# The MLP's second product by Strassen's seven products, over all features, in rings of buffers

## The chip, the cores and the metric

The kernel runs on 1 core of one Trainium2 chip. The metric is the device time of one execution in microseconds (us). A difference of about 0.3% is what a measurement of this kernel can tell from none.

## The reference

Two layers act on 1024 tokens of width 1024, all in float32. Each layer is a token mixer, a cross-attention into 256 memory tokens and a squared-ReLU MLP, each followed by a layer norm of a scaled residual. The change is in the MLP:

```python
def squared_relu_mlp(x, w1, w2):
    h = jnp.square(jax.nn.relu(jnp.einsum('bsd,df->bsf', x, w1)))
    return jnp.einsum('bsf,fd->bsd', h, w2)

for l in range(DEPTH):      # DEPTH = 2
    ...
    ff = squared_relu_mlp(x, w_ff1[l], w_ff2[l])
    x = layer_norm(ALPHA * x + ff, ln3_g[l], ln3_b[l])
```

Here `x` is 1024 x 1024, `w1` is 1024 x 4096 and `w2` is 4096 x 1024.

## The kernel before

Every float32 factor is split into two fp32r parts, a high and a low one: ScalarE copies the high part, and VectorE or GpSimd subtracts it to get the low part (`split`, L648 on the line of the subtraction). `mm3` (L333 to L335) then adds three TensorE products into one PSUM bank: high by high, high by low, low by high. A bank is 128 x 512; there are eight. SBUF is handed out by an allocator of the kernel's own (`Arena`), and all loads and stores are issued by SyncE's one queue.

The stages of a layer that matter here, in order:

- `out_proj(..., "values", ...)` is the output product of the cross-attention, token tile by token tile (8 tiles of 128 tokens). It ends each tile with a layer norm (`layer_norm`, L620 and L623 on VectorE).
- `x_combos` takes each normed tile, stores it to DRAM (`x2`), transposes it on TensorE (L1522) and makes the token-side operands of the first product: B11 and B21 from tiles 0 to 3 alone, and B22, T1, T2, T3, T4 from tile t and tile t - 4 together (L1540 to L1550 on VectorE, the splits of T1 to T3 on GpSimd).
- `up` is the first product, h = relu(w1 x) squared, already by Strassen's algorithm with Winograd's sums: 16 chunks of 256 features, seven products of 12 matmuls each (`PRODUCTS`). Products 1 and 2 need B11 and B21 only. The order is: 1 and 2 of the first four chunks (`UP_FIRST`), then 6, 5, 7, 3, 4 of these, then the other chunks whole. The weights are loaded by chunk and summed (S1 to S4, L1581); VectorE adds the products (L1672), ScalarE squares, and four 128 x 512 tiles per chunk are stored to `h` in DRAM.
- `mlp` then makes the second product plainly. For each of 8 groups of 512 features, `fetch` loads four 128 x 1024 rows of h and splits them (L1694 ScalarE, L1695 VectorE), the weights of w2 come through a small prefetcher (L283 to L285), and `down(g, t, d)` makes 12 matmuls into one bank and adds them to the residual tile (L1737 in group 0, L1741 after). In the last group it goes tile by tile, so that the layer norms of one tile run beside the products of the next.

What is written is not what runs in order: a scheduler places each engine's instructions by priorities, so that the program's order of one engine is a result of it. The orders below are those of the built programs.

## Time and profile before

| | |
|---|---|
| median of 3 runs | 3144.88 us (3141.48 to 3149.49) |
| profiled execution | 3145.91 us |
| its span | 3144.1 us |
| TensorE busy | 2979.4 us, 95% of the span, 14824 matmuls |
| VectorE busy | 1913.4 us, 61% |
| ScalarE, GpSimd busy | 1410.7 us (45%), 1367.0 us (43%) |
| mean granted TensorE clock | 0.973 of full |

In the profile PE is TensorE's matmuls, PEld its weight loads, DVE VectorE, ACT ScalarE, POOL GpSimd and SP SyncE. Matmuls are pipelined: one of 128 x 512 shows about 390 ns, but the next one starts 0.23 us after it, so the pace is read from counts over a stretch, not from mean durations. The profiled execution took 3145.91 us, 1.8 us more than its span.

### The profile page before, as it was taken

To read this page: it belongs to the slowest core of one execution; us is meant where nothing else is said; L and a number is where in the kernel's file an instruction comes from. 1 tells how busy PE (TensorE), PEld (TensorE's weight loads), DVE (VectorE), ACT (ScalarE), POOL (GpSimd) and SP (SyncE) were. 2 spreads that over 40 slices of the span, in tenths; PEclk is the share of its full clock that TensorE was granted. 3 is DMA by queue.
4 is the path that set the end of the run, shared out by engine and by line. 5 is a ranking of instruction groups with operands and counts; after the bars stand their busy time and mean duration, and the time that the engine had idled before them with its cause. 6 is when DMAs were issued, how large, how long until landed. Compare 5 with 4: busy or idle time off the path is not lost. (4 is left out here: it accounts for less than half of the span.)

```text
span 3144.1 us, 42269 instructions
## 1 busy us (share of the span) xinstructions
PE 2979.4 (95%) x14824; PEld 2521.0 (80%) x14824; DVE 1913.4 (61%) x3983; ACT 1410.7 (45%) x2794; POOL 1367.0 (43%) x1292
## 2 busy tenths in 40 slices
...
DVE  5899888662675344333658998875526754443446
...
PEclk9998899999989999999999988999999899999999
...
GB/s 122 54 42 58 54 113 96 131 94 60 115 81 111 111 111 207 98 103 95 88 50 69 28 59 61 125 93 124 84 92 90 74 110 112 108 209 85 114 91 64
DMA packets 201398, 297.49 MB, mean 95 GB/s; under 512 B 16865, under 2 KB 123361, under 8 KB 201185
## 3 DMA queue, kind: packets, MB, share of 16 engines
...
## 5 line engine op out<-in xcount | busy, mean ns | idle before, releaser
L333 PE MATMUL banks<-sb,sb 128*128 128x512 f32 (+3 forms) x3904 | 1470.7, 379 | 25.6 <-DVE sb L648 11.7
L334 PE MATMUL banks<-sb,sb 128*128 128x512 f32 (+3 forms) x3904 | 1468.3, 377 | 4.6 <-POOL sb L285 4.6
L335 PE MATMUL banks<-sb,sb 128*128 128x512 f32 (+3 forms) x3904 | 1464.9, 377 | 0.5 <-POOL sb L648 0.5
L285 POOL TENSOR_TENSOR sb<-sb,sb 128x512 fp32r<-128x512 f32 (+2 forms) x416 | 572.8, 1392 | 963.0 <-ACT sb L284 674.8
L333 PEld LDWEIGHTS banks<-sb,sb 128*128 128x128 f32 x3904 | 740.3, 190 | 161.6 <-DVE sb L648 13.5
L334 PEld LDWEIGHTS banks<-sb,sb 128*128 128x128 f32 x3904 | 740.2, 190 | 133.0 <-POOL sb L285 6.4
L335 PEld LDWEIGHTS banks<-sb,sb 128*128 128x128 f32 x3904 | 739.0, 189 | 130.1 <-POOL sb L648 1.2
L648 POOL TENSOR_TENSOR sb<-sb,sb 128x512 fp32r<-128x512 f32 (+1 forms) x316 | 399.0, 1281 | 516.1 <-ACT sb L647 453.1
L284 ACT CAST sb<-sb 128x512 fp32r<-128x512 f32 (+2 forms) x320 | 190.3, 608 | 454.4 <-PE banks L335 283.1
L1741 DVE TENSOR_TENSOR sb<-banks,sb 128x512 f32<-128x512 f32 x224 | 153.4, 689 | 312.9 <-PE banks L335 311.8
L647 ACT CAST sb<-sb 128x512 fp32r<-128x512 f32 (+1 forms) x340 | 191.4, 588 | 287.9 <-PE banks L334 115.4
L1672 DVE TENSOR_TENSOR sb<-banks,sb 128x512 f32<-128x512 f32 x224 | 151.2, 688 | 230.4 <-PE banks L335 218.4
L647 ACT CAST sb<-banks 128x384 fp32r<-128x384 f32 (+2 forms) x324 | 160.6, 516 | 168.9 <-PE banks L1522 81.9
L648 DVE TENSOR_TENSOR sb<-banks,sb 128x384 fp32r<-128x384 f32 (+2 forms) x324 | 187.3, 594 | 69.3 <-ACT sb L647 65.1
L796 DVE TENSOR_SCALAR_CACHE_REDUCE sb<-sb,sb 128x768 bf16<-128x768 f32 (+3 forms) x256 | 207.4, 810 | 3.2 <-POOL sb L752 0.3
L997 POOL TENSOR_SCALAR sb<-sb,sb 128x128 f32<-128x128 f32 (+7 forms) x192 | 146.5, 778 | 75.5 <-DVE sb L995 70.4
L986 ACT ACTIVATE sb<-sb,sb 128x128 f32<-128x128 f32 (+7 forms) x192 | 141.8, 739 | 80.5 <-DVE sb L980 74.2
L792 ACT ACTIVATE sb<-sb,sb 128x1024 bf16<-128x1024 f32 (+1 forms) x128 | 140.4, 1097 | 47.0 <-DVE sb L815 45.6
L1694 ACT CAST sb<-sb 128x1024 fp32r<-128x1024 f32 x64 | 67.3, 1051 | 162.6 <-DMA sb<-h 84.3
L1057 PE MATMUL banks<-sb,sb 128*128 128x320 f32 (+4 forms) x288 | 83.1, 389 | 53.4 <-DVE sb L980 40.7
L1695 DVE TENSOR_TENSOR sb<-sb,sb 128x1024 fp32r<-128x1024 f32 x64 | 93.0, 1457 | 63.6 <-ACT sb L1694 62.6
L1634 ACT ACTIVATE sb<-sb 128x512 f32<-128x512 f32 x128 | 80.8, 631 | 111.7 <-DVE sb L1672 111.5
...
## 6 DMA issues: line engine op xcount, KB each, us to landing
sb<-w_ff_dram SPq DMA_DIRECT2D x128, 256.0 KB, 3.0
sb<-w_ff_dram SPq DMA_DIRECT2D x64, 512.0 KB, 3.8
h<-sb SPq DMA_DIRECT2D x128, 256.0 KB, 2.0
sb<-h SPq DMA_DIRECT2D x64, 512.0 KB, 4.1
sb<-w_in_dram SPq DMA_DIRECT2D x64, 256.0 KB, 2.9
sb<-w_mkv_dram SPq DMA_DIRECT2D x64, 256.0 KB, 2.7
xs<-sb SPq DMA_DIRECT2D x24, 512.0 KB, 2.6
sb<-xs SPq DMA_DIRECT2D x24, 512.0 KB, 3.9
```

What stands on the lines that cost most here:

```text
L284: (k.nc.vector.tensor_copy if self.late else k.nc.scalar.copy)(hi, st)
L285: k.nc.gpsimd.tensor_tensor(lo, st, hi.bitcast(F32), op=ALU.subtract)
L333: mm(out, lh, rh, start=start, stop=False)
L334: mm(out, lh, rl, start=False, stop=False)
L335: mm(out, ll, rh, start=False, stop=stop)
L647: nc.scalar.copy(hi, src)
L648: eng.tensor_tensor(lo, src, hi.bitcast(F32), op=ALU.subtract)
L796: nc.vector.tensor_scalar(junkb[:, :w], x, c, None, op0=ALU.is_ge, op1=ALU.add, accum_out=n)
L986: nc.scalar.activation(pt.ap, pt.ap, AF.Exp, bias=mn, scale=-1.0, accum_out=sm)
L997: nc.gpsimd.tensor_scalar(pt.ap, pt.ap, rc[:, i : i + 1], 0.0, op0=ALU.mult, op1=ALU.add)
L1672: nc.vector.tensor_tensor(r.ap, ps.ap, part[c, x].ap, op=ALU.add)
L1741: nc.vector.tensor_tensor(x, ps.ap, x, op=ALU.add)
```

## The change

The second product is made by Strassen's seven products too. It is cut in halves three ways: tokens (tiles 0 to 3 and 4 to 7), features (rows 256c to 256c + 127 and the 128 after them, for each chunk c), and output columns (512 and 512). `up` now stores, in place of the four quarters of h, the seven combinations that are the left factors of the seven products (`LEFT`): two quarters themselves and five sums or differences, made on VectorE (L1685) and stored as 128 x 512 tiles. `mlp` then goes product by product (5, 7, 3, 1, 4, 6, 2), each over all 16 chunks into four banks. Step n of 112 loads one tile of h and one of w2, adds or subtracts another quarter of w2 where the product asks for it (L1790), splits both factors (L645, which is `split`'s subtraction, L648 before) and makes 4 x 3 = 12 matmuls (four token tiles, three products each). All buffers come from rings: tiles as loaded (`raws`, 8 of 512 columns, so four steps), split pairs (`pairs`, `DOWN_AHEAD` = 7 steps) and quarters of w2 that a later product needs again (`slots`). At the end of a product its four banks are added to one or two residual tiles each (`ADDS`, L1845 and L1847). Token tiles 0 to 3 are final after product 4 and normed under product 6; the last eight steps of product 2 go tile by tile.

`UP_FIRST` is 6 instead of 4, so products 1 and 2 of six chunks come first, with small loads of their own for A11 and A12 (L1607). `out_proj` hands back the last four tiles, and their transposes and sums are called for between the first products of `up`.

```diff
-UP_FIRST = 4
+UP_FIRST = 6
+DOWN_AHEAD = 7
...
+        if hold:
+            return pend
...
+            left[c] = {"A22", "S1", "S2", "S3", "S4"}
+            if c >= UP_FIRST:
+                left[c] |= {"A11", "A12"}
...
+            early = c < UP_FIRST and n in ("A11", "A12")
+            if early:
+                b = sb.alloc(512)
+                src = b.ap.rearrange("p (k f) -> p k f", k=4)
+                i = 4 * (int(n[2]) - 1)
+                nc.sync.dma_start(src, v[:, i : i + 4, 256 * c : 256 * c + P])
...
+    LEFT = {
+        1: ("11", "+", "22"), 2: ("21", "+", "22"), 3: ("11",), 4: ("22",),
+        5: ("11", "+", "12"), 6: ("21", "-", "11"), 7: ("12", "-", "22"),
+    }
+    ADDS = {
+        1: ((0, 0, 1), (1, 1, 1)), 2: ((1, 0, 1), (1, 1, -1)), 3: ((0, 1, 1), (1, 1, 1)),
+        4: ((0, 0, 1), (1, 0, 1)), 5: ((0, 0, -1), (0, 1, 1)), 6: ((1, 1, 1),),
+        7: ((0, 0, 1),),
+    }
+
+    def h_rows(self, p, c):
+        r = ((p - 1) * (DFF // 256) + c) * P
+        return self.h[r : r + P, :]
...
-            r = 256 * c + P * f
-            nc.sync.dma_start(self.h[r : r + P, half * 512 : half * 512 + 512], b.ap)
...
+            if c < UP_FIRST and n == "11":
+
+                nc.sync.dma_start(self.h_rows(3, c), b.ap)
+                sb.free(b)
+                return
+            if c < UP_FIRST and n == "22":
+                first = quads[c, "11"] = sb.alloc(512)
+                nc.sync.dma_start(first.ap, self.h_rows(3, c))
+            quads[c, n] = b
+            have = {x for c_, x in quads if c_ == c}
+            for p, spec in self.LEFT.items():
+                names = spec[::2]
+                if (n in names or (n == "22" and c < UP_FIRST and "11" in names)) and have >= set(names):
+                    if len(names) == 1:
+                        if names[0] == n:
+                            nc.sync.dma_start(self.h_rows(p, c), b.ap)
+                        continue
+                    x, y = (quads[c, m].ap for m in names)
+                    z = sb.alloc(512)
+                    nc.vector.tensor_tensor(
+                        z.ap, x, y, op=ALU.add if spec[1] == "+" else ALU.subtract
+                    )
+                    nc.sync.dma_start(self.h_rows(p, c), z.ap)
+                    sb.free(z)
...
+            if pend and i in (0, 1, 2, 4):
+                combos(*pend.pop(0))
...
-        def fetch(g, i):
-            f = sb.alloc(1024)
-            r = (4 * g + i) * P
-            nc.sync.dma_start(f.ap, self.h[r : r + P, :])
-            b = [sb.alloc(1024) for _ in range(2)]
-            nc.scalar.copy(b[0].r, f.ap)
-            nc.vector.tensor_tensor(b[1].r, f.ap, b[0].r.bitcast(F32), op=ALU.subtract)
-            sb.free(f)
-            hs[g, i] = b
...
+        steps = [(p, i) for p in (5, 7, 3, 1, 4, 6, 2) for i in range(nk)]
...
+        def prepare(n):
+            if n >= len(steps) or n in have:
+                return
+            p, i = steps[n]
+            x, own = take(raws, 2 * n, 512)
+            y, _ = take(raws, 2 * n + 1, 512)
+            load(x, self.h_rows(p, i))
+            add = nc.vector.tensor_tensor
+            if p == 5:
+                src = load(y, w2(1, 1, i))
+                kept[i] = slots[i] if slots else sb.alloc(512)
+                nc.scalar.copy(kept[i].ap, y.ap)
+            elif p == 2:
+                src = kept.pop(i)
+            else:
+                src = y
+                row, col, op = {
+                    7: (1, 0, ALU.add), 3: (0, 1, ALU.subtract), 1: (0, 0, ALU.add),
+                    4: (1, 0, ALU.subtract), 6: (0, 1, ALU.add),
+                }[p]
+                if p == 1:
+                    new = load(slots[(i - 2) % len(slots)], w2(0, 0, i))
+                    add(y.ap, new.ap, kept[i].ap, op=op)
+                    kept[i] = new
+                else:
+                    load(y, w2(row, col, i))
+                    add(y.ap, y.ap, kept[i].ap, op=op)
+            res = []
+            for j, (b, eng) in enumerate(
+                ((x, nc.gpsimd if i % 2 else nc.vector), (src, nc.vector))
+            ):
+                hl, _ = take(pairs if n < nlast else None, 2 * n + j, 1024)
+                self.split(hl.r[:, :512], hl.r[:, 512:], b.ap, eng=eng)
+                res.append(hl)
+            if not own:
+                sb.free(x)
+                sb.free(y)
+            if p == 2:
+                slots.remove(src)
+                sb.free(src)
+            have[n] = res
...
+        pairs += [b for n in range(first) for b in have[n]]
+        pairs += [sb.alloc(1024) for _ in range(2 * (DOWN_AHEAD - first))]
+        raws += [sb.alloc(512) for _ in range(8)]
+        slots += [kept[i] for i in range(first)]
+        slots += [sb.alloc(512) for _ in range(nk + 2 - first)]
...
-        def down(g, t, d):
-            ps = self.ps.alloc()
-            for i in range(4):
-                u = self.wi[f"f2_{g}", l][4 * d + i]
-                hi, lo = self.w.get(u)
-                h = hs[g, i]
-                self.mm3(ps.ap, h[0].r[:, s], h[1].r[:, s], hi, lo, i == 0, i == 3)
...
+        def product(n, t, ps):
+            i = steps[n][1]
+            x, y = (b.r for b in have[n])
             s = slice(t * P, (t + 1) * P)
+            self.mm3(
+                ps[t].ap, x[:, :512][:, s], x[:, 512:][:, s], y[:, :512], y[:, 512:],
+                i == 0, i == nk - 1,
+            )
...
+        def evict(p, t, ps):
+            for half, d, sign in self.ADDS[p]:
+                tt = 4 * half + t
+                x = xs[tt].ap[:, d * 512 : d * 512 + 512]
+                op = ALU.add if sign > 0 else ALU.subtract
+                if (tt, d) in begun:
+                    nc.vector.tensor_tensor(x, x, ps[t].ap, op=op)
+                else:
+                    nc.vector.scalar_tensor_tensor(
+                        x, x, ALPHA, ps[t].ap, op0=ALU.mult, op1=op
+                    )
+                    begun.add((tt, d))
...
+        for n, (p, i) in enumerate(steps[:nlast]):
+            for m in range(n, min(2 * n + 5, n + DOWN_AHEAD)):
+                prepare(m)
+            if p in (5, 7) and i in (6, 8, 10, 12):
+                t = i // 2 - 3 + (0 if p == 5 else 4)
+                nc.sync.dma_start(xs[t].ap, self.x2[t * P : (t + 1) * P, :])
+            if p == 3 and i == 0:
+                self.ln_consts("ln3_g", "ln3_b", l, gb)
+            if i == 0:
+                ps = [self.ps.alloc() for _ in range(4)]
+            for t in range(4):
+                product(n, t, ps)
+            drop(n)
+            if i == nk - 1:
+                for t in range(4):
+                    evict(p, t, ps)
+            if p == 6:
+                if i % 4 == 2:
+                    norm(i // 4, 0)
...
+        for n in range(nlast, len(steps)):
+            prepare(n)
...
+        for t in range(4):
+            for n in range(nlast, len(steps)):
+                product(n, t, ps)
+                if t == 3:
+                    drop(n)
+            evict(2, t, ps)
+            norm(4 + t, 2 if t < 1 else int(t < 3))
```

TensorE, at the start of layer 0's `up`, before. L1522 are the transposes of the last token tiles (`sb_67` is the identity), the rows around them the last matmuls of `out_proj` and the first of product 1:

```order
L333 MATMUL banks<-sb_673,sb_178 128x512
L334 MATMUL banks<-sb_673,sb_178 128x512
L335 MATMUL banks<-sb_673,sb_5643 128x512
L1522 MATMUL banks<-sb_67,sb_7490 128x128 x8
L1522 MATMUL banks<-sb_67,sb_3604 128x128 x8
L1522 MATMUL banks<-sb_67,sb_1853 128x128 x8
L333 MATMUL banks<-sb_86,sb_2723 128x512
L334 MATMUL banks<-sb_93,sb_2723 128x512
```

The same place now (L340 to L342 are `mm3`, L1521 the transposes), here the end of the first product and the second of the four tiles:

```order
L340 MATMUL banks<-sb_86,sb_1731 128x512
L341 MATMUL banks<-sb_93,sb_1731 128x512
L342 MATMUL banks<-sb_86,sb_1731 128x512
L1521 MATMUL banks<-sb_67,sb_3604 128x128 x8
L340 MATMUL banks<-sb_169,sb_310 128x512
L341 MATMUL banks<-sb_7550,sb_310 128x512
L342 MATMUL banks<-sb_169,sb_310 128x512
```

Before, tiles 4, 5 and 6 are transposed in one piece behind `out_proj`, then come 48 matmuls, then tile 7. Now tile 4 follows `out_proj`, tiles 5 and 6 come after 12 matmuls each, and tile 7 after 74 more, 98 in all.

VectorE, around the end of the layer norm of token tile 7 (L623, its last operation, and L589 and L591 before it), before. L1581 are sums of weights, L648 splits, L1672 sums of products, L1540 the first operation on the transposed tile 7:

```order
L1581 TENSOR_TENSOR sb_905<-sb_4403,sb_195 128x512
L648 TENSOR_TENSOR sb_7831<-sb_3887,sb_7830 128x4x128
L589 TENSOR_SCALAR sb_2510<-sb_2510 128x1
L648 TENSOR_TENSOR sb_7831<-sb_7871,sb_7830 128x4x128
L1672 TENSOR_TENSOR sb_2551<-banks,sb_4592 128x512
L591 TENSOR_SCALAR sb_2510<-sb_2510 128x1
L1581 TENSOR_TENSOR sb_4403<-sb_2195,sb_7490 128x512
L589 TENSOR_SCALAR sb_2510<-sb_2510 128x1
L591 TENSOR_SCALAR sb_2510<-sb_2510 128x1
L623 SCALAR_TENSOR_TENSOR sb_1937<-sb_1937,sb_2510,sb_135 128x1024
L1581 TENSOR_TENSOR sb_2551<-sb_2111,sb_905 128x512
L1540 TENSOR_TENSOR sb_2690<-banks,sb_86 128x512
```

The same place now (L620 is the norm's last operation, L645 the splits, L1582 the sums of weights, L1727 the sums of products, L1539 the first operation on tile 7):

```order
L645 TENSOR_TENSOR sb_177<-banks,sb_170 128x4x128
L586 TENSOR_SCALAR sb_2510<-sb_2510 128x1
L1549 TENSOR_TENSOR sb_842<-sb_842,sb_7550 128x512
L588 TENSOR_SCALAR sb_2510<-sb_2510 128x1
L645 TENSOR_TENSOR sb_7830<-sb_7861,sb_7829 128x4x128
L620 SCALAR_TENSOR_TENSOR sb_5765<-sb_5765,sb_2510,sb_135 128x1024
L645 TENSOR_TENSOR sb_7830<-sb_842,sb_7829 128x4x128
L1727 TENSOR_TENSOR sb_842<-banks,sb_7910 128x512
L1582 TENSOR_TENSOR sb_7963<-sb_163,sb_2111 128x512
L1539 TENSOR_TENSOR sb_901<-banks,sb_86 128x512
L1582 TENSOR_TENSOR sb_8083<-sb_7963,sb_163 128x512
L1542 TENSOR_TENSOR sb_901<-sb_901,sb_93 128x512
```

Before, three sums of weights stand between tile 7's last products and the end of its norm; now none does, and one of the three splits of T4 has moved behind the norm too.

VectorE in the second product of layer 0, before: sums into the residual (L1741) and splits of fetched rows of h (L1695):

```order
L1741 TENSOR_TENSOR sb_9930<-banks,sb_9930 128x512
L1695 TENSOR_TENSOR sb_1747<-sb_149,sb_1731 128x1024
L1741 TENSOR_TENSOR sb_9932<-banks,sb_9932 128x512
L1695 TENSOR_TENSOR sb_4838<-sb_10741,sb_3222 128x1024
L1741 TENSOR_TENSOR sb_9922<-banks,sb_9922 128x512
L1695 TENSOR_TENSOR sb_5442<-sb_1763,sb_7222 128x1024
```

The same engine now, under product 6 of layer 0: sums of w2 (L1790), splits (L645) and, between them, the norms of token tiles 0 to 3 (L604 to L617):

```order
L617 SCALAR_TENSOR_TENSOR sb_7489<-sb_7489,sb_2510,sb_10747 128x1024
L604 BN_AGGR sb_2510<-sb_2510 128x2
L1790 TENSOR_TENSOR sb_3520<-sb_3520,sb_842 128x512
L645 TENSOR_TENSOR sb_629<-sb_2551,sb_629 128x512
L604 BN_AGGR sb_2510<-sb_2510 128x2
L1790 TENSOR_TENSOR sb_10137<-sb_10137,sb_905 128x512
L579 TENSOR_SCALAR sb_2510<-sb_2510 128x1
L581 TENSOR_SCALAR sb_2510<-sb_2510 128x1
L617 SCALAR_TENSOR_TENSOR sb_5317<-sb_5317,sb_2510,sb_10747 128x1024
L645 TENSOR_TENSOR sb_729<-sb_901,sb_729 128x512
```

The operations with a PSUM operand (`banks`) have become rare there, and most of what VectorE now does has both inputs in SBUF (`sb`).

## Rows read from the trace of the kernel before

**Rows 1.** The page: busy time, then the span in 40 equal slices (tenths busy of VectorE, and the granted TensorE clock in tenths).

```profile
PE 2979.4 (95%) x14824; PEld 2521.0 (80%) x14824; DVE 1913.4 (61%) x3983; ACT 1410.7 (45%) x2794; POOL 1367.0 (43%) x1292
...
DVE  5899888662675344333658998875526754443446
...
PEclk9998899999989999999999988999999899999999
```

**Rows 2.** The view by stretches, in the MLP's two products of both layers: the stretch, its length, then busy time and count of instructions of each engine, the granted clock, the DMA share and GB/s.

```profile
950.00:1180.00 230.00, 230.00 (x1016) 190.51 (x1015) 100.72 (x140) 117.05 (x197) 112.19 (x88) 1.00 0.34 112
1260.00:1500.00 240.00, 240.00 (x1060) 198.80 (x1059) 91.50 (x110) 47.44 (x65) 69.65 (x47) 1.00 0.28 96
2510.00:2750.00 240.00, 240.00 (x1061) 198.72 (x1060) 108.72 (x148) 123.44 (x208) 121.01 (x93) 1.00 0.33 110
2810.00:3080.00 270.00, 270.00 (x1193) 223.58 (x1192) 100.91 (x123) 55.97 (x76) 76.17 (x51) 1.00 0.27 91
```

**Rows 3.** The same view around the start of `up`, in layer 0, layer 1, and two pieces of the first.

```profile
872.00:940.00 68.00, 50.42 (x219) 40.99 (x218) 54.85 (x75) 27.74 (x50) 39.61 (x26) 0.87 0.23 74
2440.00:2510.00 70.00, 50.14 (x202) 39.55 (x201) 49.14 (x67) 28.85 (x51) 38.24 (x25) 0.80 0.22 75
908.00:912.00 4.00, 0.00 (x0) 0.00 (x0) 4.00 (x8) 2.31 (x5) 0.82 (x2) 0.65 0.42 133
912.00:916.00 4.00, 0.00 (x0) 0.00 (x0) 3.49 (x7) 1.75 (x3) 2.55 (x2) 0.50 0.35 131
```

**Rows 4.** The view of waits of TensorE, from 872 to 940 us (first two) and from 2440 to 2510 us (last): who waited for whom, us in total, times, longest.

```profile
PE banks L1522 <- DVE sb L623: 10.4, 1, 10.4
PE banks L333 <- DVE sb L648: 5.7, 1, 5.7
...
PE banks L1522 <- DVE sb L623: 10.0, 1, 10.0
```

**Rows 5.** The timeline of layer 0 between `out_proj` and `up`: start, length, engine, line, and in brackets the idle time before and what ended it.

```profile
883.78 1.37 DVE L1300 SCALAR_TENSOR_TENSOR sb<-sb,banks 128x512 f32<-128x512 f32 x2 [3.55 <-PE banks L335]
884.27 2.78 PE L1522 MATMUL banks<-sb,sb 128*128 128x128 f32 x24
...
890.54 17.80 POOL L648 TENSOR_TENSOR sb<-sb,sb 128x512 fp32r<-128x512 f32 x11 [1.25 <-ACT sb L647]
...
915.56 1.28 DVE L623 SCALAR_TENSOR_TENSOR sb<-sb,sb,sb 128x1024 f32<-128x1024 f32 x1
...
916.90 1.97 PE L1522 MATMUL banks<-sb,sb 128*128 128x128 f32 x8 [10.39 <-DVE sb L623]
```

**Rows 6.** Groups of instructions by line from 890.5 to 907 us, where VectorE and GpSimd both run without a pause: count, busy time, mean ns of one.

```profile
L1549 DVE TENSOR_TENSOR sb<-sb,sb 128x512 f32<-128x512 f32 x3 | 4.1, 1362 | 0.0
...
L1545 DVE TENSOR_TENSOR sb<-banks,sb 128x512 f32<-128x512 f32 x3 | 2.0, 674 | 0.0
...
L648 POOL TENSOR_TENSOR sb<-sb,sb 128x512 fp32r<-128x512 f32 x11 | 17.8, 1653 | 1.2 <-ACT sb L647 1.2
```

**Rows 7.** Operations of one kind: the view of line L1581 over the whole span (ns, least/median/most), and groups by line from 950 to 1180 us (L1672, L1581, L648, L647) and from 1260 to 1500 us (L285).

```profile
L1581 DVE TENSOR_TENSOR sb<-sb,sb x96: 676/693/1807, 905.4 to 2748.1; 128x512 f32<-128x512 f32 x96
...
L1672 DVE TENSOR_TENSOR sb<-banks,sb 128x512 f32<-128x512 f32 x88 | 59.5, 689 | 92.8 <-PE banks L335 91.5 <-ACT sb L1635 1.2
L1581 DVE TENSOR_TENSOR sb<-sb,sb 128x512 f32<-128x512 f32 x39 | 31.6, 811 | 24.6 <-DMA h<-sb 12.8 <-ACT sb L1634 8.5 <-ACT sb L1635 2.7
...
L648 POOL TENSOR_TENSOR sb<-sb,sb 128x512 fp32r<-128x512 f32 x88 | 114.3, 1318 | 117.8 <-ACT sb L647 117.8
...
L647 ACT CAST sb<-sb 128x512 fp32r<-128x512 f32 x88 | 52.4, 621 | 61.3 <-PE banks L334 44.1 <-DVE sb L1581 14.5 <-DMA h<-sb 2.3
...
L285 POOL TENSOR_TENSOR sb<-sb,sb 128x512 fp32r<-128x512 f32 x47 | 70.8, 1531 | 169.6 <-ACT sb L284 139.4 <-issue 17.3 <-PE banks L334 12.7
```

**Rows 8.** VectorE's groups from 1530 to 1580 us, where layer 0's last norms run: the pieces of a norm, and of a transposed tile's split (L639).

```profile
L596 DVE BATCH_NORM_STATS2 sb<-sb 128x6 f32<-128x512 f32 x14 | 9.6, 688 | 0.1
...
L639 DVE TENSOR_TENSOR sb<-banks,sb 128x512 fp32r<-128x512 f32 x12 | 8.1, 683 | 0.5 <-ACT sb L638 0.5
L589 DVE TENSOR_SCALAR sb<-sb 128x1 f32<-128x1 f32 x23 | 6.1, 266 | 0.3
L591 DVE TENSOR_SCALAR sb<-sb 128x1 f32<-128x1 f32 x23 | 4.8, 208 | 0.3
...
L607 DVE BATCH_NORM_AGGREGATE sb<-sb 128x2 f32<-128x12 f32 x8 | 1.6, 203 | 0.1
```

**Rows 9.** DMA issues with KB each and median us to landing: from 1260 to 1500 us (first two), and the busiest stretch, from 1190 to 1240 us (its rate, then two issues).

```profile
sb<-w_ff_dram SPq DMA_DIRECT2D x47, 256.0 KB, 2.8
sb<-h SPq DMA_DIRECT2D x20, 512.0 KB, 3.4
...
DMA packets 5447, 15.20 MB, mean 304 GB/s; under 512 B 601, under 2 KB 601, under 8 KB 5445
...
sb<-x SPq DMA_DIRECT2D x8, 512.0 KB, 8.6
sb<-w_ff_dram SPq DMA_DIRECT2D x11, 256.0 KB, 6.0
```

**Rows 10.** The timeline at the end of the kernel: the last matmul, and VectorE's last operation on the last token tile.

```profile
3130.91 0.39 PE L335 MATMUL banks<-sb,sb 128*128 128x512 f32 x1
...
3139.22 1.28 DVE L623 SCALAR_TENSOR_TENSOR sb<-sb,sb,sb 128x1024 f32<-128x1024 f32 x1
```

177 lines of the change are left out of this document (83 added, 94 removed).

## The prediction

> **What bounds the kernel now.** I read the page first, then the view by stretches, then the waits and the timeline where that view shows a hole. The page has TensorE at 95% and VectorE at 61% [rows 1]. By stretches, TensorE is busy all the time in both products of the MLP, in both layers, at a granted clock of 1.00, and the pace is the same everywhere: 240 us / 1060 = 0.2264 us per 128 x 512 matmul, also 230 / 1016 and 270 / 1193 [rows 2]. VectorE is at 38 to 45% there. So in the MLP the end moves with the number of matmuls, as long as nothing else becomes late. There is one hole per layer, between `out_proj` and `up`: the stretches of 68 and 70 us hold 219 and 202 TensorE instructions at clocks of 0.87 and 0.80 [rows 3]. 32 of each are transposes at 2.78 / 24 = 0.116 us [rows 5]. Work there is 187 x 0.2264 + 3.7 = 46.0 us and 170 x 0.2264 + 3.7 = 42.2 us, so 22.0 and 27.8 us are lost. The waits name the cause: TensorE stands 10.4 and 10.0 us before tile 7's transposes, for the end of its layer norm on VectorE [rows 4], which runs without a pause from tile 7's products at 883.78 to that end at 916.84 [rows 5]. After eight idle microseconds the clock is at 0.50, the lower of its levels, 1.2 GHz [rows 3].
>
> **A. Fewer matmuls.** Before, 8 groups x 16 x 12 = 1536 per layer; now 7 x 16 x 12 = 1344. In two layers 384 x 0.2264 = 86.9 us go, since TensorE had no pause there [rows 2].
>
> **B. The hole.** In the new order tile 7's transposes stand behind 24 others (2.8 us) and 98 matmuls (22.2 us), so at the earliest at 884.3 + 25.0 = 909.3. On VectorE three sums of weights and one split of T4 have left the way to the norm's end; with GpSimd at work beside them they took 1.36 each, and one without it 0.69 [rows 6, 7]: 3 x 1.36 + 0.69 = 4.8 us, so the norm ends at about 912. GpSimd decides a little too. The eighth weight pair's split stands behind eight of the nine splits of T1 to T3; the last of these waits for VectorE's 27th operation, at some 907, and at 1.65 us each [rows 6] the pair is ready near 912, where TensorE wants it at 906. So TensorE stops for 5 to 6 us there instead of 10 + 6 later, and the 46 matmuls left (10.4 us) then cover tile 7's sums. With 3 to 4 us at the lower clock I take 10 us lost in layer 0 and 13 in layer 1 (its hole is a quarter deeper). Gain: 12 + 14.8 = 27 us. Bounds: 0 (the hole moves to the next wait) and 42 us (4 left in each).
>
> **C. VectorE under product 6.** This is the change's dearest new place, because the norms of tiles 0 to 3 now run among the splits. An operation on 512 columns takes 0.69 us with a PSUM input [rows 7] and as much at its median without [rows 7], but 1.36 where GpSimd runs beside it, while those with PSUM stay at 0.67 [rows 6]. A GpSimd split of 1.65 us covers 1.65 / 1.36 = 1.2 such operations, so it costs VectorE up to 1.2 x 0.67 = 0.8 us. A plain step pair in the second product is 2 sums, 3 splits and its share of 8 sums into the residual (one): 6 x 0.69 + 0.8 = 4.9 us against TensorE's 24 x 0.2264 = 5.43. So VectorE follows, and gets the full lead of six steps. From the sums after product 4 to the last split before the tile-by-tile end, the new order holds on VectorE 40 splits, 9 sums of w2 and 12 sums into the residual (61 x 0.69 = 42.1), four norms at 0.69 + 0.2 + 4 x 0.27 + 4 x 0.21 + 2 x 1.28 = 5.4 [rows 5, 8] (21.5), and in layer 0 six splits of transposed tiles at 0.68 [rows 8] (4.1): 67.7 us, with 13 GpSimd splits at 0.8 78.1. TensorE needs the last of these after 24 steps and seven eighths of a tile's pass: 24 x 2.717 + 4.3 = 69.5. It waits 8.6 us in layer 0 and 4.5 in layer 1: +13. Bounds: 0 (VectorE undisturbed: 67.7 is in time) and +27 (below).
>
> **D. Under `up`.** VectorE gets five sums per chunk. In the first six chunks' products 6, 5, 7, 3, 4 it has 4 + 6 + 5 = 15 operations and GpSimd 5 splits: 10.4 + 4.0 = 14.4 us against 60 x 0.2264 = 13.6, so 0.8 x 6 x 2 = +9. In the other chunks 16 operations and 7 splits, 16.6 against 19.0: covered. Waits for buffers that a store still reads were 12.8 us over 39 sums before [rows 7], hidden by VectorE's free time; with seven stores per chunk instead of four there will be more, and I add 3. +12, bounds 0 and +65 (below). ScalarE's added casts (0.62 us [rows 7], two per step of 2.72) stay hidden.
>
> **E. The ends.** Product 2 adds both column halves of a tile after its last matmul, where before one half was done earlier. At the kernel's end one more sum and one more statistic come after the last matmul (0.69 + 0.69 [rows 7, 8]), ahead of the norm that ends the kernel [rows 10]: +1.4. The seam between the layers keeps its order in the main: 0, bounds -4 and +4.
>
> **F. Loads.** A step loads 512 KB in 2.72 us, 193 GB/s. Before the second product moved 91 to 96 GB/s [rows 2] and its loads landed in 2.8 and 3.4 us [rows 9]. A loaded tile's slot comes round after four steps, 10.9 us; with a landing of 3.4, sum, cast and split (0.69 + 0.62 + 0.69 = 2.0, or 0.62 + 1.53 = 2.2 on GpSimd [rows 7]) and a wait of 2.4 in VectorE's queue (half a step pair) it needs 8 us. Cost 0.
>
> **Sum.** -86.9 - 27 + 13 + 12 + 1.4 = -87.5 us. The profiled execution's own 3145.9 us become 3058.4; the median of before lies 1.0 under that execution, so 3057 us. The forecast's own range, with either B halved or C and D doubled, or the reverse, is 3032 to 3082.
>
> **Rivals.**
>
> *VectorE is locked out by GpSimd.* A two-input operation of VectorE may have to wait for the whole GpSimd split, 1.32 us [rows 7], not 0.8. Then product 6 needs 67.7 + 13 x 1.32 = 84.9: 15.4 and 11.3 us late, 27 in all. The first six chunks need 10.4 + 6.6 = 17.0 against 13.6, +40; the others 11.0 + 9.2 = 20.2 against 19.0, +25 over both layers; the plain step pairs 4.1 + 1.3 = 5.46 against 5.43, +2. That is 94 in place of C's 13 and D's 9: 3057 + 72 = 3129 us. For it: the slowest L1581 took 1.81 us, 1.1 above its least [rows 7]. Against it: 1.36 on average with GpSimd running all the time [rows 6]. The Trainium skill ("SBUF — State Buffer", section "Who interferes with whom") states this rule: a VectorE instruction with two SBUF inputs and a GpSimd instruction that reads SBUF exclude each other for a whole instruction. By that rule, the trace agrees in that only operations without a PSUM input are slowed, and not in the size: where GpSimd never stops it would make the mean 0.69 + 1.32 = 2.0 us, and 1.36 was measured [rows 6].
>
> *The hole only moves.* If tile 7's sums are late again after the norm, B is 0: 3084 us. For it: VectorE has no pause from 884 to 912 [rows 3, 5] and the new order removes only 4.9 us of its work. Against it: TensorE has 48 more matmuls ready.
>
> *The ring of four loaded steps starves TensorE (slower).* Where loads came at 304 GB/s, a 512 KB tile landed in 8.6 us and a 256 KB one in 6.0 [rows 9]. A slot needs its landing + 4.4 us (2.0 of work, 2.4 in the queue), and up to a landing of 6.5 us that is within 10.9. At 8.6 a step takes 13.0 / 4 = 3.25 us, 0.53 more, over 104 steps in two layers: +111 us, 3167 us, slower by 0.7%. For it: SyncE has one queue, and stores and loads wait in it. Against it: the rate is 193 GB/s, not 304, and tiles are 256 KB.
>
> *The change does not do what it says* can be left out: the new order has 384 fewer matmuls of 128 x 512.
>
> **Chances.** The forecast 0.66, VectorE locked out 0.15, the hole moves 0.13, the ring 0.06. A measurement of this kernel can tell 0.3%, 9.4 us, from no change: faster means under 3135.5. The forecast and the moved hole lie below, and five sixths of VectorE's case; of the ring's nearly all lies above: faster 0.91, within 0.3% 0.03, slower 0.06. The range is 3028 (B's upper end and no C or D: 3145.9 - 86.9 - 42 + 1.4 = 3018, seldom whole) to 3112, which leaves out the ring and most of VectorE's case.
>
> **What would show it.** A: 14440 matmuls, and 0.226 us per matmul in both products at clock 1.00. B: the stretch from `out_proj`'s end to product 6 with 10 us lost and the wait for the norm's end (L620) gone or under 5 us; a wait of `mm3` for GpSimd's L645 in its place. C: TensorE waiting for L645 on VectorE only near the end of product 6 and in product 2, more in layer 0. D: VectorE at 90% or more in the first six chunks, 70 to 85% after. F: loads of `h` landing in under 5 us. I am wrong if VectorE is at 95% in the middle of the second product (locked out), or if sums (L1790) wait for loads of w2 (the ring).

## The result and the profile after

The changed kernel takes 3056.04 us (median of 4 runs, 3054.18 to 3057.68), beside 3143.98 us for the kernel before in the same comparison: ratio 0.9718, interval 0.9701 to 0.9735. The forecast was 3057 us. The profiled execution took 3054.18 us, its span is 3052.4.

The page of the kernel after, in the form of [rows 1]:

```profile
PE 2894.9 (95%) x14440; PEld 2452.0 (80%) x14440; DVE 2239.0 (73%) x4423; ACT 1527.2 (50%) x3074; POOL 1317.6 (43%) x1260
...
DVE  5899978672478776777858998785725877667787
...
PEclk9999899999999999999999998999999999999999
```

14440 matmuls, as forecast; VectorE went from 61 to 73%, TensorE stayed at 95%. The clock's dips at the two holes, the 8 in the 12th and in the 32nd slice of [rows 1], are gone.

The view by stretches of the kernel after, in the form of [rows 2]. The first two stretches run from the MLP's first product into its second, in layer 0 and in layer 1. Then come the start of `up` as in [rows 3] and 200 us from the same point on (12.3 us ahead of tile 4's transposes), in layer 0 and in layer 1:

```profile
1060.00:1300.00 240.00, 240.00 (x1061) 198.72 (x1060) 166.30 (x217) 129.03 (x222) 96.39 (x72) 1.00 0.60 206
2560.00:2950.00 390.00, 390.00 (x1722) 322.94 (x1721) 284.86 (x379) 193.79 (x336) 145.44 (x102) 1.00 0.58 197
...
878.60:946.60 68.00, 62.67 (x274) 50.63 (x273) 59.39 (x79) 34.27 (x61) 45.97 (x31) 0.95 0.37 120
878.60:1078.60 200.00, 191.63 (x835) 156.91 (x834) 161.98 (x203) 95.30 (x166) 113.92 (x78) 0.97 0.46 156
2394.40:2464.40 70.00, 64.28 (x283) 52.18 (x282) 59.33 (x80) 34.10 (x62) 46.70 (x31) 0.95 0.36 117
2394.40:2594.40 200.00, 189.28 (x822) 154.86 (x821) 158.99 (x202) 92.98 (x163) 111.64 (x76) 0.97 0.46 154
```

The same 200 us of the kernel before, from 12.3 us ahead of its tile 4's transposes:

```profile
872.00:1072.00 200.00, 182.42 (x801) 150.34 (x800) 118.00 (x159) 95.70 (x163) 108.13 (x78) 0.96 0.30 100
2434.20:2634.20 200.00, 180.14 (x776) 147.18 (x775) 114.29 (x157) 94.03 (x160) 104.97 (x75) 0.93 0.28 95
```

The pace in the products is unchanged: 240 / 1061 and 390 / 1722 are 0.226 us per matmul at a clock of 1.00, with VectorE at 69 to 73%. At the start of `up` the 68 and 70 us hold 274 and 283 instructions, not 219 and 202; the 200 us hold 34 and 46 more.

The view of waits of TensorE after, from 870 to 1080 us, beside [rows 4]:

```profile
PE banks L340 <- DVE sb L645: 3.8, 3, 2.2
PE banks L342 <- POOL sb L645: 3.0, 1, 3.0
PE banks L340 <- DVE sb L1727: 1.5, 1, 1.5
```

The wait for the norm's end (L623 then, L620 now) is gone; three short waits for splits by VectorE and one for GpSimd stand in its place.

To see where the time went over the whole span I cut every run at four marks that the timeline and the view of one line give: tile 4's transposes (L1521, before L1522) and the last sum into the residual (L1845, before L1741), in each layer. The stage between the MLPs (the seam and layer 1's mixer and cross-attention) has no line that the runs change, but for `out_proj`'s order of giving buffers back and, with the later transposes, the place of the seam's transposes. In us, one execution each:

| kernel | to tile 4, layer 0 | MLP, layer 0 | between | MLP, layer 1 |
|---|---|---|---|---|
| before | 884.3 | 684.4 | 877.8 | 684.8 |
| after | 890.9 | 638.8 | 877.0 | 632.4 |
| old start | 894.9 | 640.7 | 883.9 | 634.7 |
| old start, whole loads | 892.1 | 646.9 | 884.7 | 635.9 |
| four pairs | 893.2 | 638.0 | 891.0 | 630.7 |
| constants given back late | 886.2 | 638.1 | 877.7 | 628.1 |
| later transposes | 889.3 | 639.1 | 866.0 | 632.0 |
| S4's split on VectorE | 890.2 | 640.4 | 880.3 | 632.4 |
| constants and transposes | 884.9 | 636.9 | 868.2 | 632.2 |
| the same, four pairs | 882.5 | 636.9 | 880.3 | 627.7 |
| all h splits on GpSimd | 889.8 | 641.6 | 880.5 | 632.3 |
| no h split on GpSimd | 891.3 | 641.5 | 877.4 | 631.5 |
| three steps in the ring | 890.2 | 655.9 | 882.7 | 654.5 |
| two steps in the ring | 891.2 | 678.7 | 886.9 | 673.6 |

How much of such a difference is only that of two executions can be read where kernels run the same lines in the same order on every engine. Up to layer 0's tile 4 seven do (the kernel after, later transposes, S4's split, both GpSimd runs, both rings): 889.3 to 891.3 us. Between the MLPs four do (the kernel after, S4's split, all on GpSimd, three steps): 877.0 to 882.7. In layer 0's MLP two do (the kernel after, constants late): 638.8 and 638.1. So differences of up to 6 us in the third column, 2 in the first and about 1 in the others say nothing by themselves.

From before to after the two MLPs lose 45.6 + 52.4 = 98.0 us, the stage ahead of the first grows by 6.6, the stage between shrinks by 0.8, and the rest at the end grows by 0.5: -91.7, the difference of the spans of the two profiled executions. The medians differ by 87.9.

Two pieces of the change have no run of their own. In the second product the allocator now takes the lowest place that was given back at least 24 steps of its own clock ago, not 6, and the next layer's first weights are called for beside the last tiles. What they are worth in these columns is not known.

### The profile page after: what moved, and what is told of

Read it like the earlier page. It is cut to its first block, busy times and chain, and to the rows that moved or that the text cites. A ratio compares the mean times of both kernels' runs of the same rounds, so it can differ in the third digit from the quotient of the medians.

```text
span 3052.4 us, 43458 instructions
## 1 busy us (share of the span) xinstructions
PE 2894.9 (95%) x14440; PEld 2452.0 (80%) x14440; DVE 2239.0 (73%) x4423; ACT 1527.2 (50%) x3074; POOL 1317.6 (43%) x1260
## 5 line engine op out<-in xcount | busy, mean ns | idle before, releaser
L340 PE MATMUL banks<-sb,sb 128*128 128x512 f32 (+3 forms) x3776 | 1427.2, 379 | 31.8 <-DVE sb L645 11.7
L341 PE MATMUL banks<-sb,sb 128*128 128x512 f32 (+3 forms) x3776 | 1421.4, 377 | 6.0 <-POOL sb L286 5.9
L342 PE MATMUL banks<-sb,sb 128*128 128x512 f32 (+3 forms) x3776 | 1419.5, 377 | 6.5 <-POOL sb L645 6.5
L645 POOL TENSOR_TENSOR sb<-sb,sb 128x512 fp32r<-128x512 f32 (+1 forms) x428 | 588.1, 1386 | 946.1 <-ACT sb L644 834.9
L340 PEld LDWEIGHTS banks<-sb,sb 128*128 128x128 f32 x3776 | 717.0, 190 | 164.0 <-DVE sb L645 14.9
L342 PEld LDWEIGHTS banks<-sb,sb 128*128 128x128 f32 x3776 | 717.1, 190 | 132.0 <-POOL sb L645 7.3
L341 PEld LDWEIGHTS banks<-sb,sb 128*128 128x128 f32 x3776 | 717.6, 190 | 128.7 <-POOL sb L286 7.5
L644 ACT CAST sb<-sb 128x512 fp32r<-128x512 f32 (+1 forms) x788 | 452.5, 605 | 580.1 <-PE banks L341 135.1
L286 POOL TENSOR_TENSOR sb<-sb,sb 128x512 fp32r<-128x512 f32 (+2 forms) x288 | 376.3, 1319 | 512.0 <-ACT sb L285 403.7
L645 DVE TENSOR_TENSOR sb<-sb,sb 128x512 fp32r<-128x512 f32 x360 | 285.8, 821 | 41.6 <-ACT sb L644 41.3
L645 DVE TENSOR_TENSOR sb<-banks,sb 128x384 fp32r<-128x384 f32 (+2 forms) x324 | 187.8, 595 | 80.8 <-ACT sb L644 76.1
L644 ACT CAST sb<-banks 128x384 fp32r<-128x384 f32 (+2 forms) x324 | 160.0, 516 | 172.1 <-PE banks L1521 75.2
L1685 DVE TENSOR_TENSOR sb<-sb,sb 128x512 f32<-128x512 f32 x160 | 158.4, 1025 | 56.9 <-ACT sb L1665 53.9
L1727 DVE TENSOR_TENSOR sb<-banks,sb 128x512 f32<-128x512 f32 x224 | 149.8, 683 | 45.9 <-PE banks L342 40.4
L983 ACT ACTIVATE sb<-sb,sb 128x640 f32<-128x640 f32 (+7 forms) x192 | 141.7, 739 | 77.5 <-DVE sb L977 73.2
L285 ACT CAST sb<-sb 128x512 fp32r<-128x512 f32 (+2 forms) x192 | 112.0, 599 | 125.9 <-PE banks L341 29.2
L1790 DVE TENSOR_TENSOR sb<-sb,sb 128x512 f32<-128x512 f32 x128 | 97.9, 767 | 70.5 <-DMA sb<-w_ff_dram 69.8
L1582 DVE TENSOR_TENSOR sb<-sb,sb 128x512 f32<-128x512 f32 x96 | 91.6, 954 | 50.7 <-DMA h<-sb 30.7
```

The costliest lines, as they stand in the source:

```text
L286: k.nc.gpsimd.tensor_tensor(lo, st, hi.bitcast(F32), op=ALU.subtract)
L340: mm(out, lh, rh, start=start, stop=False)
L341: mm(out, lh, rl, start=False, stop=False)
L342: mm(out, ll, rh, start=False, stop=stop)
L644: nc.scalar.copy(hi, src)
L645: eng.tensor_tensor(lo, src, hi.bitcast(F32), op=ALU.subtract)
```

## The experiments

All times are medians, with the ratio to the kernel before and its interval.

### The start of `up`: old start, four pairs, whole loads

The first undoes both edits to the start, the second the two more pairs alone:

```diff
-UP_FIRST = 6
+UP_FIRST = 4
...
-                l, "values", ot, self.xs[0], "ln2_g", "ln2_b", then, hold=True
+                l, "values", ot, self.xs[0], "ln2_g", "ln2_b", then, hold=False
```

> The changed kernel with the start of `up` as before: four pairs first, and all transposes and sums called for in `out_proj`. Theory (the start is a gain of its own, 27 us forecast, about 31 us read from the two traces): the hole before tile 7's transposes is back, 20 to 28 us lost in each layer, and the time is 3056 + 27 to 31, less some 3 us for two chunks per layer that are no longer early, so 3080 to 3087 us. Rival (the hole only moves, the whole gain is the matmuls): 3054 to 3059 us.

> The changed kernel with four pairs first instead of six, but the last four tiles still handed back and called for between the first products. Theory (both halves are needed: moving the tiles takes the norm out of VectorE's queue jam, and the two more pairs, 48 matmuls or 10.9 us per layer, cover tile 7's sums): 8 to 10 us more lost per layer, 3070 to 3076 us. Rival (the move alone does it): 3053 to 3057 us. Second rival (the pairs alone do it): as the old start, 3080 us or more.

Measured: 3066.46 us (0.9755, 0.9737 to 0.9772) for the old start and 3067.23 us (0.9761, 0.9745 to 0.9776) for four pairs. Both theories on the first fail: the old start costs 10 us, not 27 or none, and of these 1.9 + 2.3 lie in the MLPs. The stretches of the old start:

```profile
882.60:950.60 68.00, 56.36 (x240) 45.53 (x239) 56.75 (x77) 28.54 (x50) 38.77 (x26) 0.90 0.33 105
882.60:1082.60 200.00, 188.36 (x823) 154.84 (x822) 161.17 (x202) 94.96 (x165) 113.12 (x77) 0.97 0.45 150
2407.20:2477.20 70.00, 56.27 (x238) 44.15 (x237) 54.37 (x80) 30.42 (x54) 42.15 (x28) 0.90 0.31 95
2407.20:2607.20 200.00, 186.27 (x812) 151.81 (x811) 152.72 (x201) 93.77 (x163) 112.20 (x77) 0.97 0.45 148
```

In the hole it stands 34 and 45 instructions behind the kernel after (240 and 238 to 274 and 283), 17.9 us at 0.2264. But over the 200 us only 12 and 10 behind (823 and 812 to 835 and 822), 5.0 us. So 12.9 of the 17.9 us are given back within the next 130 us; the hole and the loss under the first chunks are one account, not two.

The four pairs' stretches:

```profile
880.90:948.90 68.00, 60.20 (x263) 48.99 (x263) 61.83 (x85) 31.99 (x58) 45.68 (x29) 0.92 0.34 108
880.90:1080.90 200.00, 191.48 (x839) 157.10 (x839) 161.15 (x203) 95.09 (x166) 114.25 (x77) 0.97 0.45 148
2409.90:2479.90 70.00, 59.81 (x257) 48.62 (x256) 64.53 (x85) 32.64 (x58) 45.47 (x29) 0.93 0.31 100
2409.90:2609.90 200.00, 189.81 (x831) 156.25 (x830) 159.48 (x204) 97.31 (x168) 115.18 (x79) 0.97 0.45 148
```

Fewer instructions than after in the hole, but 4 and 9 more over the 200 us (2.9 us), and the MLPs are shorter by 0.8 and 1.7 us. So here handing the tiles back is what gained (839 and 831 instructions to the old start's 823 and 812), and the fifth and sixth pair cost some 2.5 to 2.9 us, little more than two executions can differ by. That this kernel is slower by 11 us comes from the stage between, 14.0 us longer (891.0 to 877.0), whose lines its edit does not touch. Of the 14.0, 4.2 are one wait of TensorE for L636 in layer 1, which the kernel after does not have there; the rest was not followed.

The third goes on from the old start and loads whole chunks ahead of products 1 and 2 again:

```diff
-            early = c < UP_FIRST and n in ("A11", "A12")
+            early = False
...
-            if c >= UP_FIRST:
-                left[c] |= {"A11", "A12"}
+            left[c] |= {"A11", "A12"}
...
-            if not (c_ < UP_FIRST and p_ in (1, 2)):
-                load(c_)
+            load(c_)
```

> The run with the old start, and also with whole chunks loaded ahead of products 1 and 2 as before, no small loads of A11 and A12. Theory (the 13 us that the old start still gained on the kernel before, near `up`'s begin, come from the small loads: without whole chunks the weight sums leave VectorE's queue ahead of tile 7's norm): the 200 us stretches fall from 823 and 812 TensorE instructions to about 801 and 776, the wait for tile 7's norm (L620) grows from 6.3 to about 10 us, and the time is 3066 + 13 = 3075 to 3083 us. Rival (it is the second product's w2 loads and splits that no longer run ahead there): counts and time as with the old start, 3062 to 3070 us.

Measured: 3074.43 us (0.9782, 0.9768 to 0.9796), just under the theory's range, but for half its reason. Its stretches of 200 us:

```profile
879.80:1079.80 200.00, 183.44 (x802) 149.78 (x801) 151.53 (x197) 92.29 (x159) 107.57 (x74) 0.96 0.39 132
...
2411.40:2611.40 200.00, 187.33 (x813) 152.35 (x813) 153.04 (x197) 91.41 (x160) 112.76 (x75) 0.97 0.40 134
```

In layer 0 the count falls from 823 to 802, that of the kernel before (801); in layer 1 it stays (812, 813), where the kernel before had 776. The small loads were worth 21 instructions, 4.8 us, in layer 0 and nothing in layer 1. The waits do not follow the theory either. In layer 0 TensorE no longer waits for the norm but for splits, 8.2 us for L645 on VectorE and 6.2 for L644. In layer 1 the wait for the norm (L620) grows from 4.5 to 7.0 us, and the count stays all the same. What made layer 1's start 37 instructions (8.4 us) better with everything at the start undone was not tried.

### The front of layer 0: constants given back late

```diff
-        for x in gb:
-            sb.free(x)
-        if hold:
-            return pend
-        for x_ in pend:
-            then(*x_)
+        if not hold:
+            for x_ in pend:
+                then(*x_)
+        for x in gb:
+            sb.free(x)
+        if hold:
+            return pend
```

> The changed kernel with one thing put back in `out_proj`: the two rows of layer norm constants are given back after the pending tiles' work, as before, and not ahead of it. Theory (the front of layer 0 is 6.6 us longer after the change because buffers fall elsewhere and the scheduler's order changes with them): 640 to 700 us in layer 0 goes back to 298 TensorE instructions from 259, and the time is 3045 to 3051 us. Rival (the loss there has another cause): 3054 to 3058 us, and the stretch keeps its wait for L636.

Measured: 3045.01 us (0.9684, 0.9671 to 0.9697). The stretch from 640 to 700 us, of the kernel before, of the kernel after, and of this one:

```profile
640.00:700.00 60.00, 60.00 (x298) 50.37 (x297) 35.77 (x74) 18.06 (x35) 20.73 (x16) 1.00 0.27 96
```

```profile
640.00:700.00 60.00, 55.71 (x259) 46.40 (x258) 34.93 (x70) 15.64 (x28) 18.89 (x14) 0.94 0.25 88
```

```profile
640.00:700.00 60.00, 60.00 (x294) 50.34 (x293) 36.97 (x76) 17.02 (x33) 20.70 (x16) 1.00 0.30 105
```

The theory holds: 4.7 us come back ahead of layer 0's MLP, and the wait for L636 (the split of a transposed tile; 4.3 us, the only wait of the stretch) is gone. Another 4.3 us come in layer 1's MLP (628.1 to 632.4), though not when the later transposes are added (632.2, below). All that the edit changes is when a buffer is given back, and the order of the instructions behind it is another one. That this comes about through the places that the next tiles get is argued, not shown.

### Product 6: later transposes

```diff
-            if pend:
-                then(*pend.pop())
+            if len(pend) > (1 if t < 4 else 0):
+                then(*pend.pop(0))
             self.layer_norm(xs[t].ap, gb, spread, st)
+            if t == 4:
+                then(*pend.pop(0))
```

> The changed kernel with the transposes of tiles 0 to 3 called for one norm later than now. Theory (what is lost near the end of product 6 in layer 0, about 4 us, is TensorE standing at transposes for the norms' ends, L620): the wait L628 for L620 goes and the time is 3051 to 3053 us. Rival, the forecast's own reason (VectorE's splits are late under product 6): the wait moves to L340 for L645 and the time stays 3055 to 3058 us.

Measured: 3041.42 us (0.9672, 0.9659 to 0.9686): faster than expected, and not for the reason given. TensorE's timeline near the end of product 6 in layer 0, of the kernel after and of this one:

```profile
1472.36 1.28 PE L628 MATMUL banks<-sb,sb 128*128 128x128 f32 x8 [2.73 <-DVE sb L620]
1473.80 1.97 PE L628 MATMUL banks<-sb,sb 128*128 128x128 f32 x8 [0.16 <-DVE sb L620]
1482.54 1.25 PE L628 MATMUL banks<-sb,sb 128*128 128x128 f32 x8 [0.89 <-DVE sb L636]
```

```profile
1473.39 1.09 PE L628 MATMUL banks<-sb,sb 128*128 128x128 f32 x8 [3.22 <-DVE sb L620]
```

The wait for the norm stays (3.2 us in place of 2.9), and the MLP of layer 0 takes 639.1 us, not less than 638.8. Against the forecast's own reason the rows speak too: no wait of L340 for L645 in either. The gain is 11.0 us in the stage between (866.0 to 877.0, twice what one order varies by), where the moved transposes change the order from the seam on; which of that stage's waits went was not followed further.

### GpSimd's price to VectorE: all h splits on GpSimd, none on GpSimd

```diff
-                ((x, nc.gpsimd if i % 2 else nc.vector), (src, nc.vector))
+                ((x, nc.gpsimd), (src, nc.vector))
```

> The changed kernel with GpSimd taking the subtraction of every h tile's split in the second product, not of every other one. A plain step pair is then 5 VectorE operations (3.45 us at 0.69) beside two GpSimd splits. Forecast's price (a GpSimd split costs VectorE 0.8 us): 3.45 + 1.6 = 5.05 us against TensorE's 5.43, TensorE still busy all the time in the second product, 3052 to 3060 us. Rival (locked out, 1.32 us of GpSimd apart from VectorE's two-input work in SBUF): 3.45 + 2.64 = 6.09 us per pair, 0.66 more than TensorE, over some 50 pairs in each of two layers about 65 us: 3120 us, with VectorE at 95% or more and TensorE waiting for L645.

> The changed kernel with all splits of the second product's h tiles on VectorE. A plain step pair is 7 VectorE operations, 4.83 us at 0.69, with nothing of GpSimd beside them, against 5.43: TensorE busy all the time there, the time 3050 to 3060 us by both theories. What it measures is VectorE's time per step without GpSimd: at 0.69 per operation by both; with the run that gives every split to GpSimd, the price of a GpSimd split to VectorE, 0.8 (forecast), 1.32 (locked out) or 0 (no contention).

Measured: 3059.96 us (0.9727, 0.9711 to 0.9743) with all, 3057.05 us (one run) with none. The stretches 1100 to 1400 and 2650 to 2950 us, of the kernel after, with all, and with none:

```profile
1100.00:1400.00 300.00, 300.00 (x1325) 248.42 (x1324) 211.08 (x294) 148.19 (x256) 104.26 (x73) 1.00 0.60 204
2650.00:2950.00 300.00, 300.00 (x1325) 248.43 (x1324) 218.92 (x300) 147.20 (x257) 95.70 (x67) 1.00 0.61 208
```

```profile
1100.00:1400.00 300.00, 300.00 (x1325) 248.43 (x1324) 221.74 (x258) 148.58 (x256) 156.04 (x111) 1.00 0.60 204
2650.00:2950.00 300.00, 300.00 (x1326) 248.39 (x1325) 217.20 (x256) 145.84 (x256) 155.69 (x111) 1.00 0.62 206
```

```profile
1100.00:1400.00 300.00, 300.00 (x1325) 248.41 (x1324) 223.88 (x335) 149.90 (x259) 50.11 (x37) 1.00 0.61 206
2650.00:2950.00 300.00, 300.00 (x1325) 248.39 (x1325) 226.90 (x348) 147.79 (x259) 35.25 (x26) 1.00 0.63 211
```

TensorE has no pause in any of the three, and VectorE is at 73% with all splits on GpSimd: the rival's sum (95% or more, 3120 us) is out. Two unknowns, two sums: 683 VectorE operations and 63 of GpSimd made VectorE busy for 450.8 us, 514 and 222 for 438.9. That is 0.61 us per operation and 0.57 us more for each of GpSimd's, which take 1.40 (311.7 / 222). Put into the kernel after, 594 x 0.61 + 140 x 0.57 gives 442 us against 430.0, so the price is rough: the other two pairs of the three runs give 0.45 and 0.66.

A price of two fifths of a split does not mean that the two engines share. The timeline of the run with all splits on GpSimd shows one locking out the other:

```profile
1271.68 1.74 POOL L645 TENSOR_TENSOR sb<-sb,sb 128x512 fp32r<-128x512 f32 x1
1272.20 1.77 DVE L645 TENSOR_TENSOR sb<-sb,sb 128x512 fp32r<-128x512 f32 x1
...
1273.66 1.46 POOL L645 TENSOR_TENSOR sb<-sb,sb 128x512 fp32r<-128x512 f32 x1 [0.24 <-ACT sb L644]
```

VectorE's operation starts while a GpSimd split runs and ends 0.55 us after it (1273.97 to 1273.42). The next split starts while that operation runs and ends 1.15 us after it (1275.12). Alone an operation shows 0.68 us and a split 1.30. In the two stretches of that run, 153 VectorE operations with two SBUF inputs start under a running split, and 142 of them end 0.53 to 0.57 us after the split's end; 42 with a PSUM input start under one and show 0.68 us as ever. The 153 show 1.43 us on average, so 0.75 x 153 / 220 = 0.52 us per split, near the price above. It is lower than a split's length because an operation comes at any point of a split and waits only for what is left of it, and because 69 of the 220 splits have none starting under them. The Trainium skill ("SBUF — State Buffer", section "SBUF: two separate sides") says that whichever of the two starts first holds the shared ports for the whole instruction while the other is blocked; by that rule the trace agrees. So the mean of 2.0 us, by which the prediction found that the size did not fit the rule, did not follow from it.

### The ring of loaded tiles: three steps, two steps

```diff
         raws += [sb.alloc(512) for _ in range(8)]
+        spare = raws[6:]
+        del raws[6:]
...
-        for b in raws + slots:
+        for b in raws + spare + slots:
```

(4 in place of 6 for two steps.)

> The changed kernel with three steps in the ring of loaded tiles, not four (the other two buffers are kept, and unused). By the forecast's sum a slot is held for the landing, here 3.1 us, and 4.4 us of work and queue, 7.5 us; three steps come round in 8.15 us: no change, 3053 to 3060 us, with more waits of ScalarE and VectorE for loads. If a slot is held longer than 8.15 us, TensorE loses a third of the excess per step over some 104 steps in each layer: at 9 us 0.28 us per step, 3115 us.

> The changed kernel with two steps in the ring of loaded tiles (the other four buffers are kept, and unused). By the forecast's sum, 7.5 us held and 5.43 us round: a step takes 3.75 us instead of 2.72, over some 104 steps in each of two layers 215 us more, 3270 us. If the 2.4 us in VectorE's queue that the sum counts fall away when VectorE has less to do, 5.1 us are held, and the time stays within 3053 to 3065 us.

Measured: 3098.54 us (0.9853, 0.9838 to 0.9867) with three steps, 3146.10 us (one run) with two. Neither number is the forecast's sum. The stretches 1350 to 1400 and 1450 to 1500 us with three steps:

```profile
1350.00:1400.00 50.00, 47.95 (x211) 39.05 (x210) 35.27 (x52) 20.15 (x34) 16.79 (x9) 1.00 0.55 172
...
1450.00:1500.00 50.00, 40.14 (x170) 31.36 (x168) 48.36 (x91) 21.44 (x39) 12.44 (x8) 0.93 0.52 169
```

and TensorE's longest wait in it from 1300 to 1510 us:

```profile
PE banks L341 <- DVE sb L645: 12.9, 7, 4.1
```

With two steps the two MLPs lose 39.9 + 41.2 = 81.1 us over some 208 steps, 0.39 per step: a slot is held 2 x (2.72 + 0.39) = 6.2 us on average, less than the 7.5 of the sum. By that three steps (8.15 us) would do, and they do in the first three products of the second product (x220 in 1300 to 1350 us, x222 in the kernel after). From product 1 on they do not (x211 in 1350 to 1400 us, x222 in the kernel after), and least of all under product 6, where VectorE has norms to do (x170 in 1450 to 1500 us, x204 after). So the hold is not one number; the loss is largest where VectorE has most to do. Four steps lose nothing before product 6, and three lose 39 us in the two MLPs: the ring has a margin of less than one step. Why products 1 and 4 already lose with three was not settled.

### Under the first six chunks: S4's split on VectorE

```diff
-            self.split(hi, lo, src, eng=nc.gpsimd)
+            self.split(hi, lo, src, eng=nc.vector if c < UP_FIRST and n == "S4" else nc.gpsimd)
```

> The changed kernel with one of the five weight splits per chunk in the first six chunks' products 6, 5, 7, 3, 4 (that of S4) on VectorE instead of GpSimd. Theory (what is lost under these chunks, 4.7 and 7.5 us, is TensorE waiting for GpSimd's splits, 3.0 and 3.4 us of it): these waits go, and the 200 us from 12.3 us ahead of tile 4's transposes, which held 835 and 822 TensorE instructions, hold 10 to 15 more; 3049 to 3053 us. Rival, the forecast's own reason (VectorE is the engine that runs short there): VectorE has 16 operations per chunk instead of 15, the counts stay or fall, 3055 to 3062 us.

Measured: 3056.43 us (0.9726, 0.9710 to 0.9742), the same as without the edit. TensorE's two longest waits in it from 877 to 1078 us:

```profile
PE banks L340 <- DVE sb L645: 5.3, 3, 2.2
PE banks L342 <- POOL sb L645: 3.4, 1, 3.4
```

The counts of 200 us are 831 and 822 (835 and 822 without). The wait for GpSimd stays (3.0 us without the edit, 3.4 with it) although GpSimd has a fifth less to do there, so the theory falls. Time and counts are those that the rival forecast, but they don't bear out its reason: six more operations per layer, 3.7 us at 0.61, cost 4 instructions and none, 0.9 us, so VectorE has time to spare there. The kernel after shows in the timelines of GpSimd, VectorE and SyncE what stands ahead of that wait (at 1005 us):

```profile
1002.01 7.71 POOL L645 TENSOR_TENSOR sb<-sb,sb 128x512 fp32r<-128x512 f32 x5 [6.49 <-ACT sb L644]
```

```profile
997.60 0.69 DVE L1582 TENSOR_TENSOR sb<-sb,sb 128x512 f32<-128x512 f32 x1 [3.23 <-DMA sb<-w_ff_dram]
```

```profile
993.40 0.38 SPq L1570 DMA_DIRECT2D sb<-w_ff_dram  x1
993.89 0.45 SPq L1681 DMA_DIRECT2D h<-sb  x1
994.40 0.41 SPq L1688 DMA_DIRECT2D h<-sb  x1
994.90 0.43 SPq L1570 DMA_DIRECT2D sb<-w_ff_dram  x1
```

GpSimd was idle for 6.5 us and then has five splits at once; VectorE was idle for 3.2 us before a weight sum, for a chunk's load, which SyncE issued among stores of h only at 993.4 and 994.9. By these rows the load was late, not an engine. No run here changed the queue, so that is argued, not shown.

### The edits that helped, together

The constants given back late and the later transposes, with six pairs and with four:

> The two edits that made it faster, together: the norm constants given back after the pending work, and the transposes of tiles 0 to 3 one norm later. If what they do in their own places adds up (5.4 us at layer 0's front, 3 us at the end of its product 6, 4 us at layer 1's hole) and the stages that neither touches keep the changed kernel's time: 3042 to 3046 us. If layer 1's token mixer, which was 10 to 13 us shorter with the later transposes and the same with the constants, goes with the transposes: 3032 to 3038 us. If the mixer's time is a matter of how its instructions happen to fall, anything from 3032 to 3055 us.

> The same two edits with four pairs first instead of six. With four pairs (and the tiles still handed back) the stretch around `up`'s begin was 0.9 and 2.0 us better than with six, so by stages 2 to 4 us under the other combination; with the mixer's time a matter of how instructions fall, anything from 3028 to 3055 us.

Measured: 3036.32 us (0.9661, 0.9647 to 0.9674) with six, faster than the changed kernel, and 3045.10 us (0.9687, 0.9673 to 0.9702) with four. By stages, four pairs are level in layer 0's MLP, 4.5 us ahead in layer 1's (627.7 to 632.2), and 12.1 us behind in the stage between (880.3 to 868.2). So the second of the three cases held for six pairs, where that stage went with the transposes. With four pairs it went with them too (891.0 to 880.3), but it kept what four pairs add to it: 12.1 us here, 14.0 without these two edits. Two edits that change no line of that stage moved it by about the same in both settings, and by more than the 5.7 us that one order varies by; through which waits was not followed.

## Why the prediction was right, point by point

- **A, -86.9.** Right: 14440 matmuls, the pace 0.226 and the clock 1.00 in both layers.
- **B, -27, and D, +12.** In size both were right. The first 176 TensorE instructions from tile 4's transposes on (now the 32 transposes and the first products of six chunks) took 58.6 and 64.5 us before and take 45.6 and 46.0 now: 31.5 us won. The next 360 (now products 6, 5, 7, 3, 4 of these chunks) took 81.6 us in both layers before and take 86.9 and 89.4: 13.1 lost. Together that is 18.4 us, 18.1 by the 34 + 46 instructions of the 200 us, where the forecast had 15. The norm's wait went, as forecast. But the two are one account: the old start showed that 12.9 of 17.9 us won in the hole are paid back under the chunks behind it. Of the 18.1 us the handed-back tiles and six pairs are 5.0, the small loads 4.5 (20 instructions over both layers), and 8.6, nearly all in layer 1, are left without a tried cause. The forecast gave the whole to the norm's place in VectorE's queue and to the 48 matmuls of the two more pairs. In these stretches the pairs gained nothing.
- **D's reason.** Wrong: VectorE was to be at 90% or more in the first six chunks. Over just these 360 matmuls, in layer 0 and in layer 1, VectorE is at 78 and 72%, and ScalarE and GpSimd are lower:

```profile
936.50:1023.40 86.90, 83.86 (x362) 68.87 (x360) 67.95 (x84) 38.62 (x66) 45.85 (x32) 0.98 0.54 182
2452.70:2542.10 89.40, 84.41 (x361) 69.01 (x360) 64.69 (x83) 38.17 (x66) 43.40 (x31) 0.96 0.53 177
```

With the measured prices the term's own sum is 15 x 0.61 + 5 x 0.57 = 12.0 us against 13.6: covered. So its size was right for a reason that was not; the late loads are the better candidate, not a shown one.
- **C, +13.** Mis-sized, and the waiter was another. What is left of the MLPs' 98.0 us beside A and the 18.1 is +7.0. Of these, 5.5 are in layer 0. The 1.5 in layer 1 belong to E, since TensorE has no wait there from 2595 us to its last matmul. The two prices of its sum were too high: 0.69 per operation was the length that a row shows, and 0.8 per GpSimd split measured 0.57. With 0.61 and 0.57 its sum is 37.2 + 21.5 + 3.7 + 7.4 = 69.8 us against 69.5: VectorE would be just in time. VectorE's timeline in product 6 shows the first price:

```profile
1439.86 0.68 DVE L1847 SCALAR_TENSOR_TENSOR sb<-sb,banks 128x512 f32<-128x512 f32 x1
1440.46 0.68 DVE L1845 TENSOR_TENSOR sb<-sb,banks 128x512 f32<-128x512 f32 x1
1441.06 0.68 DVE L1847 SCALAR_TENSOR_TENSOR sb<-sb,banks 128x512 f32<-128x512 f32 x1
```

Each is 0.68 long and the next starts 0.60 after it. VectorE is full there for 40 us all the same; the stretches 1440 to 1460, 1460 to 1480 and 1480 to 1500 us:

```profile
1440.00:1460.00 20.00, 20.00 (x90) 16.56 (x89) 20.00 (x38) 6.06 (x11) 5.88 (x3) 1.00 0.43 141
1460.00:1480.00 20.00, 17.11 (x77) 13.95 (x76) 20.00 (x44) 11.24 (x22) 6.62 (x4) 0.91 0.57 192
1480.00:1500.00 20.00, 18.56 (x85) 14.86 (x84) 15.49 (x23) 9.22 (x18) 5.71 (x5) 1.00 0.36 115
```

The forecast was right that VectorE is full there and wrong on what comes late. The splits go ahead, and TensorE waits for none of them. The four norms end together at 1471 to 1479 us, so TensorE stands 2.9 us at their transposes (L628 for L620) and 1.4 us for the splits of these (L636), in layer 0 alone, which has such transposes.
- **E, +1.4.** Measured 2.3: from the start of the last matmul to the end 13.2 us before (3130.91 [rows 10] to 3144.1), 15.5 after (3036.91 to 3052.4). 1.8 of them lie ahead of the last sum, in the column of layer 1's MLP, and 0.5 behind it. The seam cannot be told from the stage between.
- **F, 0.** Right: tiles of h land in 3.1 us (median of 236). The sign that was to show it wrong came all the same: 57 sums (L1790) waited for loads of w2, 69.8 us in all. They cost TensorE nothing, so the sign was badly chosen. And the case against the ring was a matter of one step.
- **Not in the sum: +6.6** ahead of layer 0's MLP. The full diff moves the lines that give the norm constants back (the pieces shown with the change leave them out), and `out_proj` runs twice in a layer; the forecast had no term for it. It made up for most of what B, C and D were better by (18.1 - 7.0 = 11.1 instead of 2). So the forecast came out 1 us off by luck: two errors, 9.1 and 6.6 us, of opposite sign. By the two profiled executions alone, which lie 3.8 us further apart than the medians, it was off by 4.

The hole that only moves is out: over the 200 us 18.1 us were won, though part of a gain in the hole does move on. The lockout is out by its price, 0.57 us per split in place of 1.32, and not as a mechanism: the rows show it. The starving ring is out by the run with four steps, which is the changed kernel itself.
